# Moving scaling rows between VectorE and ScalarE in a row-normalizing kernel, tile by tile, with more buffers for the row sums

## The chip, the cores and the metric

One core of a Trainium2 chip. The metric is the device time of one execution in microseconds, median of several. The span in a profile, from the first instruction to the last, is 1.6 to 2.1 us shorter than the time of the same execution, by an amount that hardly changes within a kernel (1.6 for before, 1.8 for after).

The names in the profile lines: DVE is VectorE, ACT is ScalarE, POOL is GpSimd; SP is SyncE, whose queue issues the loads; ACTq is the queue of ScalarE, which issues the stores. L61 is line 61 of the kernel. A transfer is *issued* when its instruction runs, and has *landed* when the last of the core's 16 DMA engines reports its part. DMA engines move packets, here 49,152 bytes each (one partition's 12 rows) or 32,768 in the last tile; a full packet is one of 49,152.

## The reference

```python
x = np.random.randn(32, 512, 1024).astype(np.float32)
sums = np.sum(np.abs(x), axis=-1, keepdims=True)
return (x / (sums + 1e-8)).astype(np.float32)
```

16,384 rows of 1,024 numbers: 67.11 MB are read and 67.11 MB written, and each row is divided by the sum of its magnitudes.

## The kernel before

Each of the 128 partitions takes 128 rows, in tiles of 12 rows (6.29 MB over all partitions), with one last tile of 8 rows (4.19 MB). There are 11 tiles, numbered 0 to 10 here. `piece` picks a tile's rows in memory. Four tile buffers go round, so load i+4 waits until store i has landed. The code below is cut at the dots.

```python
R = 12; BUFS = 4; HEAD = 32
rows = [R] * ((per_partition - HEAD) // R + 2) + [HEAD - 2 * R]   # 12 x 10, then 8
sbuf  = ctx.enter_context(tc.tile_pool(name="sbuf", bufs=BUFS))
stats = ctx.enter_context(tc.tile_pool(name="stats", bufs=4))

def normalize(x_tile, r0, k, kv):
    s = stats.tile([P, R], FP32)
    nc.vector.tensor_reduce(out=s[:, :k], in_=x_tile[:, r0:r0+k, :], ...)   # sum of magnitudes
    # ... + EPS, then inv = 1 / s ...
    nc.vector.tensor_mul(out=x_tile[:, r0:r0+kv, :], ...)    # rows 0 to kv-1 on VectorE
    for r in range(kv, k):                                   # the rest on ScalarE, row by row
        nc.scalar.activation(out=row, in_=row, func=Copy, scale=inv[:, r:r+1])

for i, k in enumerate(rows):
    x_tile = sbuf.tile([P, R, d], FP32)
    nc.sync.dma_start(out=x_tile[:, :k, :], in_=piece(x_flat, i))       # load
    if i == 0:
        normalize(x_tile, 0, k, k - 5)                                  # 5 rows on ScalarE
    else:
        normalize(x_tile, 0, k, k - 1 if i + BUFS < len(rows) else k)   # 1 row, or none
    nc.scalar.dma_start(out=piece(out_flat, i), in_=x_tile[:, :k, :])   # store
```

Of the kernel before, what the change touches and what calls it, by code (L numbers as in the profile page):

```python
# [1 line left out]

# [4 lines left out]

FP32 = mybir.dt.float32
EPS = 1e-8


@with_exitstack
def kernel(
    ctx: ExitStack,
    tc: tile.TileContext,
    x: bass.AP,
    out: bass.AP,
):
    nc = tc.nc
    P = nc.NUM_PARTITIONS  # L20

    x_flat = x.flatten_outer_dims()
    out_flat = out.flatten_outer_dims()
    n, d = x_flat.shape




    R = 12
    BUFS = 4  # L30
    HEAD = 32
    per_partition = n // P
    assert n % P == 0 and (per_partition - HEAD) % R == 0
    rows = [R] * ((per_partition - HEAD) // R + 2) + [HEAD - 2 * R]

    def piece(flat, i):
        head = flat[: P * HEAD, :].rearrange("(p r) d -> p r d", p=P)
        if i < 2:
            return head[:, R * i : R * (i + 1), :]
        if i == len(rows) - 1:  # L40
            return head[:, 2 * R :, :]
        a = P * (HEAD + R * (i - 2))
        return flat[a : a + P * R, :].rearrange("(p r) d -> p r d", p=P)

    sbuf = ctx.enter_context(tc.tile_pool(name="sbuf", bufs=BUFS))
    stats = ctx.enter_context(tc.tile_pool(name="stats", bufs=4))

    def normalize(x_tile, r0, k, kv):

        s = stats.tile([P, R], FP32)  # L50
        nc.vector.tensor_reduce(  # L51
            out=s[:, :k],
            in_=x_tile[:, r0 : r0 + k, :],
            axis=mybir.AxisListType.X,
            op=mybir.AluOpType.add,
            apply_absolute_value=True,
        )
        nc.vector.tensor_scalar_add(out=s[:, :k], in0=s[:, :k], scalar1=EPS)  # L58
        inv = stats.tile([P, R], FP32)
        nc.vector.reciprocal(out=inv[:, :k], in_=s[:, :k])  # L60
        nc.vector.tensor_mul(  # L61
            out=x_tile[:, r0 : r0 + kv, :],
            in0=x_tile[:, r0 : r0 + kv, :],
            in1=inv[:, :kv].unsqueeze(2).to_broadcast([P, kv, d]),
        )
        for r in range(kv, k):
            row = x_tile[:, r0 + r, :]
            nc.scalar.activation(  # L68
                out=row,
                in_=row,  # L70
                func=mybir.ActivationFunctionType.Copy,
                scale=inv[:, r : r + 1],
            )

    with tc.manual_schedule():
        for i, k in enumerate(rows):
            x_tile = sbuf.tile([P, R, d], FP32)
            nc.sync.dma_start(out=x_tile[:, :k, :], in_=piece(x_flat, i))  # L78


            if i == 0:
                normalize(x_tile, 0, k, k - 5)
            else:
                normalize(x_tile, 0, k, k - 1 if i + BUFS < len(rows) else k)
            nc.scalar.dma_start(out=piece(out_flat, i), in_=x_tile[:, :k, :])  # L85


# [1 line left out]
_INS = ['x']  # L89
_OUTS = [((32, 512, 1024), 'float32')]  # L90


# [23 lines left out]
```

## Time and profile before

| | before |
|---|---|
| time, median of the first three runs | 317.26 us (316.87 to 317.87) |
| span of the first profile (an execution of 318.93 us) | 317.3 us |
| VectorE busy | 268.7 us, 85% |
| ScalarE busy | 13.5 us, 4% |
| moved by DMA | 134.22 MB, both directions |
| the 16 DMA engines: share of the span that packets took | 49.6% loads, 48.9% stores |

Loads and stores together filled 98.5% of the DMA engines' time. That is the first thing to read: VectorE's 85% is high too, but it has holes, and DMA has none. The profile has three views of the same end, and they are easily confused. The chain of work says who released whom. The timeline says when a store was issued. Only the landing and packet records say when the DMA engines got to it.

### The profile page before, as it was taken

What the parts mean: (1) busy time and instruction counts of PE and PEld (TensorE: products, weight loads), DVE (VectorE), ACT (ScalarE), POOL (GpSimd) and SP (SyncE); (2) the same over time, 40 slices, a digit from 0 to 9 for tenths busy, and PEclk for the clock granted to TensorE, in tenths of its full rate; (3) what the DMA queues carried; (4) which work ended last, traced back from release to release, by engine and by line L of the source; (5) the groups of instructions that cost most, each with busy time, mean ns of one, the idle gap of its engine ahead of it and who ended that gap; (6) DMA issues with size and microseconds to landing.
All of it is one profiled execution on the core that took longest, in us unless ns stands there. A gap on an engine that the chain in (4) does not pass through costs nothing.

```text
span 317.3 us, 170 instructions
## 1 busy us (share of the span) xinstructions
DVE 268.7 (85%) x44; ACT 13.5 (4%) x12; POOL 0.2 (0%) x4
## 2 busy tenths in 40 slices
DVE  0079999999999999989995996799699969999920
ACT  0010601001000000100100010000000000000000
POOL 0000000000000000000000000000000000000000
DMA  8999999999999999999999999999999999999994
GB/s 328 465 397 471 421 378 415 415 465 409 459 434 397 477 415 415 465 409 459 428 403 477 409 428 452 409 471 415 403 477 415 428 430 452 397 477 415 403 425 215
DMA packets 3168, 134.22 MB, mean 423 GB/s; under 512 B 352, under 2 KB 352, under 8 KB 352
## 3 DMA queue, kind: packets, MB, share of 16 engines
q1 hardware_dynamic: 1584, 67.11, 49.6%
q10 hardware_dynamic: 1584, 67.11, 48.9%
HBM read 67.11 MB, written 67.11 MB: 423 GB/s over the span
## 4 chain that ended last, share of the span: by engine, by line
DVE 52%; DMA 34%; another core or an unknown queue 9%; issue 0%; SPq 0%; DVEq 0%; ACTq 0%
DVE s L51 27%; DVE x_tile L61 24%; DMA x_tile<-in_x_dram 18%; DMA out_dram<-x_tile 16%; DVE inv L60 1%; DVE s L58 0%; SPq L78 0%; DVEq L60 0%; ACTq L85 0%
## 5 line engine op out<-in xcount | busy, mean ns | idle before, releaser
L51 DVE TENSOR_REDUCE s<-x_tile 128x12 f32<-128x12288 f32 (+1 forms) x11 | 138.2, 12561 | 32.9 <-DMA x_tile<-in_x_dram 32.9
L61 DVE TENSOR_TENSOR x_tile<-x_tile,inv 128x11264 f32<-128x11264 f32 (+3 forms) x11 | 126.5, 11504 | 0.4
L68 ACT ACTIVATE x_tile<-x_tile,inv 128x1024 f32<-128x1024 f32 x11 | 12.2, 1142 | 153.6 <-DVE inv L60 153.6
L60 DVE RECIPROCAL inv<-s 128x12 f32<-128x12 f32 (+1 forms) x11 | 2.5, 226 | 0.9
L58 DVE TENSOR_SCALAR s<-s 128x12 f32<-128x12 f32 (+1 forms) x11 | 1.9, 173 | 0.4
L68 ACT ACT_TABLE_LOAD x1 | 1.3, 1283 | 17.8 <-DMA x_tile<-in_x_dram 17.8
L100 POOL MEMSET const-bfloat16-1.0<- 128x1 bf16 x1 | 0.1, 102 | 0.0
L100 POOL MEMSET const-uint8-127<- 128x1 uint8 x1 | 0.1, 102 | 0.0
L100 POOL MEMSET const-float32-0.0<- 128x1 f32 x1 | 0.1, 99 | 0.2 <-issue 0.2
L100 POOL MEMSET const-float32-1.0<- 128x1 f32 x1 | 0.1, 99 | 0.0
## 6 DMA issues: line engine op xcount, KB each, us to landing
x_tile<-in_x_dram SPq DMA_DIRECT2D x10, 6144.0 KB, 39.2
out_dram<-x_tile ACTq DMA_DIRECT2D x10, 6144.0 KB, 43.7
x_tile<-in_x_dram SPq DMA_DIRECT2D x1, 4096.0 KB, 35.4
out_dram<-x_tile ACTq DMA_DIRECT2D x1, 4096.0 KB, 13.0
```

The lines of the kernel that those rows point to most:

```text
L51: nc.vector.tensor_reduce(out=s[:, :k], in_=x_tile[:, r0 : r0 + k, :], axis=mybir.AxisListType.X, op=mybir.AluOpType.add, apply_absolute_v ...
L58: nc.vector.tensor_scalar_add(out=s[:, :k], in0=s[:, :k], scalar1=EPS)
L60: nc.vector.reciprocal(out=inv[:, :k], in_=s[:, :k])
L61: nc.vector.tensor_mul(out=x_tile[:, r0 : r0 + kv, :], in0=x_tile[:, r0 : r0 + kv, :], in1=inv[:, :kv].unsqueeze(2).to_broadcast([P, kv, d]),)
L68: nc.scalar.activation(out=row, in_=row, func=mybir.ActivationFunctionType.Copy, scale=inv[:, r : r + 1],)
L100: nc = _bacc.Bacc("TRN2", target_bir_lowering=False, num_devices=1)
```

## The change

ScalarE's help moves to both ends of the kernel: three rows instead of one on tiles 1 and 2, two and three on the last two tiles, none in the middle. The intent is to issue early stores and the last stores sooner. The row sums get one buffer a tile, so that no tile waits for the sums of an earlier one to be read.

```diff
-    stats = ctx.enter_context(tc.tile_pool(name="stats", bufs=4))
+    stats = ctx.enter_context(tc.tile_pool(name="stats", bufs=len(rows)))
...
+    last = len(rows) - 1
+    scalar_rows = {0: 5, 1: 3, 2: 3, last - 1: 2, last: 3}
...
-            if i == 0:
-                normalize(x_tile, 0, k, k - 5)
-            else:
-                normalize(x_tile, 0, k, k - 1 if i + BUFS < len(rows) else k)
+            normalize(x_tile, 0, k, k - scalar_rows.get(i, 0))
```

## The prediction

> **What bounds the kernel now.** I number the tiles 0 to 10 in the order of the loop: ten of 12 rows per partition (6.29 MB each way), the last of 8 rows (4.19 MB). I read the page's slices first, then the bytes by stretch, then the chain of work, then the groups and the timeline.
>
> The 40 slices of the page, and what HBM moved:
>
> ```profile
> DVE  0079999999999999989995996799699969999920
> ACT  0010601001000000100100010000000000000000
> DMA  8999999999999999999999999999999999999994
> HBM read 67.11 MB, written 67.11 MB: 423 GB/s over the span
> ```
>
> DMA is at 9 in every slice but the first and the last; VectorE has holes from the middle on; ScalarE is nearly empty. Next, the stretches (after the range: its length, busy time of VectorE, ScalarE, GpSimd, the clock, the DMA share, GB/s):
>
> ```profile
> 32.00:40.00 8.00, 8.00 (x2) 4.52 (x5) 0.00 (x0) 1.00 0.91 393
> 40.00:48.00 8.00, 8.00 (x1) 0.00 (x0) 0.00 (x0) 1.00 1.05 387
> 192.00:224.00 32.00, 27.52 (x5) 0.00 (x0) 0.00 (x0) 1.00 1.02 441
> 288.00:302.00 14.00, 13.83 (x4) 0.00 (x0) 0.00 (x0) 1.00 1.04 449
> 302.00:306.00 4.00, 1.17 (x1) 0.00 (x0) 0.00 (x0) 1.00 0.66 279
> 306.00:314.00 8.00, 0.00 (x0) 0.00 (x0) 0.00 (x0) 1.00 0.94 406
> ```
>
> These rates wobble because a packet is 49 KB. Spreading each packet record over its own duration gives, in slices of 8 us, 433.6 to 434.1 GB/s nearly everywhere, whether loads run alone, both directions, or stores alone; a full packet takes 1815 ns on its DMA engine. So 134.22 MB at 433.8 GB/s is 309.4 us that no instruction order shortens. The first packet starts at 1.73 us: together 311.1. The other 6.2 us of the 317.3 us span, by my addition over the packet records: 0.9 slow first packets, 1.3 slow packets when the first store starts (40 to 48 us: 365 instead of 433.8 GB/s), about 0.4 scattered slow ones, 0.5 a gap before the last store, 1.8 DMA engines that finish unevenly (13 of 16 near 313.9, the last at 315.88), 1.4 after the last packet.
>
> The chain of work tells another story, and one must not fall for it:
>
> ```profile
> 258.85 12.96 DVE s L51
> 272.38 12.96 DVE x_tile L61
> 285.33 8.61 DVE s L51
> 294.48 8.69 DVE x_tile L61
> ```
>
> It follows releases: load 9 lands at 258.83, VectorE works through tiles 9 and 10, the last store is issued at 303.2 and lands at 316.23. It doesn't show that this store then queues behind the one before. The landing records do: store 9 has its last landing at 306.56, store 10 at 316.23. The 9.67 us between are exactly 4.19 MB at 433.8 GB/s. The DMA engine that ends last had no idle time before store 10.
>
> **What the Trainium skill says.** "DMA: Bandwidth & Descriptors", section "Where 436 GB/s comes from", puts the ceiling of the fabric at 435.2 GB/s; 433.8 measured agrees. The same section says that about 358 GB/s of HBM binds such transfers; this trace disagrees. "SBUF — State Buffer", section "Who interferes with whom", says that neither ScalarE nor a DMA contends with VectorE. The trace agrees for ScalarE: the multiply of 7 rows beside five ScalarE rows took 7626 ns, and 12 rows without took 12958, which is 1066 ns a row at one fixed cost. "ScalarE: Activation LUTs", section "What ACT_TABLE_LOAD costs", gives 280 + 0.833 N ns for an activation with one per-partition pointer operand, so 1133 for 1024 elements, and 93 ns of overlap back to back; the trace has 1142, and five in 5.30 us. [...]
>
> **The change part by part.** The prices are in these groups:
>
> ```profile
> L61 DVE TENSOR_TENSOR x_tile<-x_tile,inv 128x11264 f32<-128x11264 f32 x6 | 71.4, 11892 | 0.2
> L61 DVE TENSOR_TENSOR x_tile<-x_tile,inv 128x12288 f32<-128x12288 f32 x3 | 38.9, 12958 | 0.1
> L68 ACT ACTIVATE x_tile<-x_tile,inv 128x1024 f32<-128x1024 f32 x11 | 12.2, 1142 | 153.6 <-DVE inv L60 153.6
> ```
>
> Rows on ScalarE were 5 on tile 0, one on each of tiles 1 to 6, none after. They become 5, 3, 3, then none on 3 to 8, 2 on tile 9, 3 on tile 10: 16 instead of 11. VectorE loses five rows in all, 5 x 1.066 = 5.3 us of its 268.7; ScalarE gains 5.5.
>
> - Tile 0: nothing changes. Its store is still issued at 38.9 and still meets the slow packets after it.
> - Tiles 1 and 2: two rows fewer, multiply 11.89 - 2.13 = 9.76 us; ScalarE's three rows (about 3.3) lie beside it. Store 1 is issued at 62.1 instead of 64.19, store 2 at 85.2 instead of 89.45. But store 0 lands only at 73.29 and store 1 at 102.3; the queue is full, and the stores land when they did. Loads 4 to 6, which wait for these landings to get their buffers back, do not move either.
> - Tile 3: its load landed at 82.87, VectorE is ready at 85.1; multiply 12.96 instead of 11.89; store 3 at about 111.5 instead of 114.7. Tile 4 then waits some 0.5 us for its load (111.87); store 4 at about 138.4 instead of 140.0.
> - Tiles 5 and 6: they start where their loads land (141.07, 170.20), which does not move. The multiply is 1.07 longer, so stores 5 and 6 are issued at 167.7 and 196.8 instead of 166.6 and 195.7. Stores 4 and 5 before them land at 189.3 and 218.3, so there are over 20 us of reserve: 0 us.
> - Tiles 7 and 8: as before.
> - Tile 9: starts with its load at 258.85; multiply 12.96 - 2.13 = 10.83; store 9 at 283.25 instead of 285.37. Store 8 lands at 292.08: 0 us.
> - Tile 10: its load's landing, about 283.0, is just earlier than VectorE's being free at 283.2. Reduction 8.68, small ones about 0.5, multiply of 5 rows 8.69 - 3 x 1.066 = 5.49; store 10 at about 298.0 instead of 303.2, 5.2 us earlier. What that is worth is the question. Thirteen of the 16 DMA engines had a gap of 0.26 to 0.89 us at 303.3 to 303.8 us, as they were done with store 9 and the last store was not there (the 279 GB/s of 302 to 306). These gaps close, 0.5 us on the average engine. The other three, with the one that ends last among them, had store 10 waiting behind store 9; for them an earlier issue changes nothing. So the end moves by 0 if that engine is equally late, and by up to 0.5 in runs where it is less so. I put 0.2.
> - Buffers of the row sums: 11 instead of 4 of each kind. VectorE's reciprocal of tile 4 and later waits for ScalarE's read of tile i-4, over long before; the trace has only an extra sequencer step of 0.07 us ahead of it. Seven of these are 0.5 us on VectorE, off the path: 0 us.
>
> Sum: 317.26 - 0.2 = 317.06, say **317.0 us**.
>
> **The rivals.** First: *the chain is right*, VectorE's tail sets the end. Then the 5.2 us at the end count in full and the time is 317.3 - 5.2 = 312 us, 1.6% faster. For it speaks the chain, which runs over VectorE from 258.85 to 303.2. Against it: 312 would leave less than a microsecond over the 311.1 of bytes and first packet, with slow packets of over 2 us and 1.4 after the last packet still to pay; and the 9.67 us between the last two landings.
> Second: *VectorE becomes the bound in the middle*, since tiles 3 to 6 get their row back: 4 x 1.07 = 4.3 us, so 321.5, 1.3% slower. Against it: VectorE's work for a full tile is then 12.95 + 12.96 + 0.6 = 26.5 us, and a tile's 12.58 MB take 29.0 us of DMA. Tiles 7 and 8 already run this way, with waits of 4.3 and 2.9 us for their loads:
>
> ```profile
> 199.95 12.95 DVE L51 TENSOR_REDUCE s<-x_tile 128x12 f32<-128x12288 f32 x1 [4.31 <-DMA x_tile<-in_x_dram]
> 229.38 12.95 DVE L51 TENSOR_REDUCE s<-x_tile 128x12 f32<-128x12288 f32 x1 [2.94 <-DMA x_tile<-in_x_dram]
> ```
>
> Third: *the moved stores change the slow packets*. The last engine's 2 us of lateness come from single slow packets near the landings of stores (187, 217, 246 us), whose cause I can't read. With stores 1 to 6 issued one to four microseconds differently, this may go either way: 316.2 to 318. I can't exclude it, and it makes most of my range.
>
> **Range and chances.** The three runs before lie within 1.0 us (316.87 to 317.87). Adding the third rival and up to 0.5 us of closed gap, I take 316.2 to 317.9. 2% is 6.3 us: faster by that would be 310.9, under the 311.1 of the bytes alone, so 0.01; slower by it would need VectorE to starve the store queue, against reserves of 9 us and more: 0.01. Within 2%: 0.98.
>
> **What would show it right or wrong.** Right: VectorE about 263.4 us busy; ScalarE 16 activations; the last store issued near 298 and taking some 18 instead of 13.0 us to land; no dip at 302 to 306; first loads' landings as before; the last landing within 0.7 us of 316.2. Wrong in the first step, if the last landing comes over 1 us earlier: then the issue of the last store did set the end. Wrong in the middle, if a store is issued later than the one before it lands, or the DMA share falls between 100 and 280 us. If the span changes by a microsecond with none of this, it is the uneven DMA engines.

## More of the kernel before

Most executions agree within a fraction of a percent; a few are one to three and a half microseconds longer.

## The result, and the profile after

After: **316.62 us** median (316.45 to 317.59, six runs). Before, with the first three runs counted in: 316.78 us (316.46 to 317.87, six runs). The ratio is **0.9998**, 95% interval 0.9976 to 1.002: the same. Ratios here are the mean time of one kernel's runs over that of the other's of the same rounds, so they are not quite the ratio of the medians quoted.

The 40 slices of the page after:

```profile
DVE  0079999999999999969996998899699969999400
ACT  0010603004000000000000000000000000202100
DMA  8999999999999999999999999999999999999996
HBM read 67.11 MB, written 67.11 MB: 425 GB/s over the span
```

ScalarE's digits have moved to the ends, VectorE's row ends about one slice earlier, and the DMA row is unchanged except for its last digit. The stretches after (columns as in the prediction: length, busy VectorE, ScalarE, GpSimd, clock, DMA share, GB/s):

```profile
40.00:48.00 8.00, 8.00 (x1) 0.00 (x0) 0.00 (x0) 1.00 1.06 393
288.00:302.00 14.00, 7.37 (x4) 3.23 (x3) 0.00 (x0) 1.00 1.01 439
302.00:306.00 4.00, 0.00 (x0) 0.00 (x0) 0.00 (x0) 1.00 0.87 377
306.00:314.00 8.00, 0.00 (x0) 0.00 (x0) 0.00 (x0) 1.00 0.92 397
```

The dip at 302 to 306 has gone from 279 to 377 GB/s, and VectorE is done by 296. (A window counts a packet where it starts. With each packet spread over its duration, 296 to 304 us has 434 GB/s after, and had 411 before.) The four big steps of the chain at the end (start, duration, what), and what the page's list of DMA issues says of the last store (size, us from issue to landing), before and then after:

```profile
256.62 12.96 DVE s L51
270.08 10.83 DVE x_tile L61
280.91 8.61 DVE s L51
289.98 5.49 DVE x_tile L61
```

```profile
out_dram<-x_tile ACTq DMA_DIRECT2D x1, 4096.0 KB, 13.0
```

```profile
out_dram<-x_tile ACTq DMA_DIRECT2D x1, 4096.0 KB, 19.3
```

Both multiplies are shorter, by 2.13 and 3.20 us, and VectorE's tail ends 7.7 us sooner than in the first profile of before; the other 2.2 to 2.4 us are tile 9's load, which landed at 256.6 instead of 258.8. The last store is issued at 295.6 instead of 303.2, and then takes 19.3 us instead of 13.0 to land. Of the 7.7 us won at the issue, 6.3 are lost in the queue.

The groups of the multiplies, with their prices (busy us, mean ns, idle before):

```profile
L61 DVE TENSOR_TENSOR x_tile<-x_tile,inv 128x12288 f32<-128x12288 f32 x6 | 77.7, 12958 | 0.4
L61 DVE TENSOR_TENSOR x_tile<-x_tile,inv 128x9216 f32<-128x9216 f32 x2 | 19.5, 9758 | 0.1
```

Nine rows cost 9758 ns, as worked out beforehand from 7, 11 and 12 rows (9.76). The middle tiles, back at 12958, still wait for their loads:

```profile
198.64 12.95 DVE L51 TENSOR_REDUCE s<-x_tile 128x12 f32<-128x12288 f32 x1 [2.55 <-DMA x_tile<-in_x_dram]
```

So this profile agrees with the explanation by bytes. But the span is 1.5 us shorter than that of the first profile, and the last landing comes at 314.9 instead of 316.2. Either the tail counted a little after all, or the first profile was of a long execution. That had to be told apart.

### The profile page after: what moved, and what is told of

It is laid out like the page before. It is cut to its first block, busy times and chain, and to the rows that moved or that the text cites. A ratio compares the mean times of both kernels' runs of the same rounds, so it can differ in the third digit from the quotient of the medians.

```text
span 315.8 us, 162 instructions
## 1 busy us (share of the span) xinstructions
DVE 263.4 (83%) x44; ACT 18.5 (6%) x17; POOL 0.2 (0%) x4
## 4 chain that ended last, share of the span: by engine, by line
DVE 42%; DMA 33%; another core or an unknown queue 18%; SPq 0%; issue 0%
DVE s L51 23%; DVE x_tile L61 18%; DMA x_tile<-in_x_dram 17%; DMA out_dram<-x_tile 16%; DVE inv L60 0%; DVE s L58 0%; SPq L83 0%
## 5 line engine op out<-in xcount | busy, mean ns | idle before, releaser
L61 DVE TENSOR_TENSOR x_tile<-x_tile,inv 128x12288 f32<-128x12288 f32 (+4 forms) x11 | 121.2, 11019 | 0.6
L68 ACT ACTIVATE x_tile<-x_tile,inv 128x1024 f32<-128x1024 f32 x16 | 17.2, 1138 | 257.0 <-DVE inv L60 257.0
## 6 DMA issues: line engine op xcount, KB each, us to landing
out_dram<-x_tile ACTq DMA_DIRECT2D x1, 4096.0 KB, 19.3
```

The costliest lines, as they stand in the source:

```text
L61: nc.vector.tensor_mul(out=x_tile[:, r0 : r0 + kv, :], in0=x_tile[:, r0 : r0 + kv, :], in1=inv[:, :kv].unsqueeze(2).to_broadcast([P, kv, d]),)
L68: nc.scalar.activation(out=row, in_=row, func=mybir.ActivationFunctionType.Copy, scale=inv[:, r : r + 1],)
```

## The experiments

Three theories. **A**: the bytes set the time, and a store only has to be issued before the one ahead of it has drained. **B**: VectorE's work or its tail sets it, as the chain suggests. **C**: what differs is the DMA engines' scattered slow packets, whatever the order. A fourth, **D**, came out of the second run. "The kernel before" in each comparison was run in the same rounds: medians 316.81, 317.16 and 317.21 us for the three groups of four kernels each (on chips 0, 12 and 7), in the order they ran.

### Only the tail of the change

```diff
-                normalize(x_tile, 0, k, k - 1 if i + BUFS < len(rows) else k)
+                normalize(x_tile, 0, k, k - {9: 2, 10: 3}.get(i, 1 if i + BUFS < len(rows) else 0))
```

> The kernel before, with only the tail of the change: ScalarE takes 2 rows of tile 9 and 3 of tile 10. Theory A (the bytes set the time; the last store only has to be issued before the store ahead of it has drained): last store issued near 298 instead of 303.2 us, time within 0.6 us of the kernel before. Theory B (the chain of work is right, VectorE's tail sets the end): about 5.2 us shorter, near 311.6.

Measured: 317.96 us, ratio 1.0045 (1.0016 to 1.0073). The last store was issued at 295.4:

```profile
295.41 0.34 ACTq L85 DMA_DIRECT2D out_dram<-x_tile  x1
```

Theory B, which wanted 311.6, is out. The time is 1.1 us over before, which is more than the 0.6 that A allowed, and in the wrong direction for B. The profiled execution (317.33 us, the shortest of the six) doesn't show the excess: its last landing, 314.4, is earlier than that of either profile of before. I come back to this under the four buffers.

### The last store later, in two steps

A 4-row, then an 8-row reduction of tile 10 whose result nobody reads goes in front of tile 10's own work, in the kernel before:

```diff
+    def burn(x_tile, m):
+        nc.vector.tensor_reduce(out=junk[:, :m], in_=x_tile[:, :m, :], ...)
...
+            if i == len(rows) - 1:
+                burn(x_tile, 4)        # 8 in the second kernel
```

> The kernel before, with a further 4-row reduction of tile 10 on VectorE, its result unused, so that the last store is issued 4.4 us later, near 307.6. Theory A: the DMA engines have drained the store before by about 303.5 to 304, so nearly all of it shows: 3.5 to 4.4 us slower, 320.3 to 321.2. Theory B: 4.4 us slower too. The run tells, with the tail-only run, whether the effect of the last store's issue has a knee: none before about 303 us, full after it.

> As the run before with 8 rows: the last store is issued 8.8 us later, near 312. Theory A: 7.9 to 8.8 us slower, 324.7 to 325.6; the step from the 4-row run is 4.3 to 4.4 us in full.

Measured: 319.39 us (ratio 1.0086, +2.6 us) and 323.57 us (1.0238, +6.8 us). The step between them is 4.2 us, as expected, but the first is 1 to 2 us too small. The traces say why: the last stores were issued at 305.1 and 309.3, not at 307.6 and 312. Without the added 4.4 us, this execution would have issued at about 300.7, not at the 303.2 of the first profile. Tile 9's load had landed at 256.4, not at 258.8. The stretch 302 to 306, from the 4-row and the 8-row run:

```profile
302.00:306.00 4.00, 3.02 (x1) 0.00 (x0) 0.00 (x0) 1.00 0.33 143
```

```profile
302.00:306.00 4.00, 4.00 (x1) 0.00 (x0) 0.00 (x0) 1.00 0.17 74
```

Now the DMA engines stand still: by the packet records, 1.9 to 2.8 us on every one of the 16 in the 4-row run, 6.0 to 7.1 in the 8-row run. In the 4-row run they were done with store 9 between 303.3 and 304.0 us, and the last store's first packet came 0.8 us after its issue. The deadline for issuing is thus about 303.3 - 0.8 = 302.5 us. An ordinary execution issues at 300.7, with 1.8 us to spare, and 4.4 - 1.8 = 2.6 us is what was measured. (That it fits to the digit is luck: the ratio's interval is 1.9 to 3.6 us wide.)

### The kernel before and the kernel after, again

> The kernel before against itself: the ratio of identical programs, 1.000, and how far it strays; two earlier runs were 0.4% over. And a second profile: if the late DMA engine of the first profile was an accident of that execution, load 9 lands near 256.4 and the last store is issued near 300.8 instead of 303.2, with no gap before it.

> The kernel after again, in the same rounds as the kernel before against itself: within 0.4% of it. If it is 0.4% faster than the run with four buffers of row sums was, relative to the kernel before, the buffers may matter; if its ratio is about 1.002 to 1.004, they do not.

Measured: 317.13 us, ratio 0.9989 (0.9948 to 1.0031) for before against itself; 316.97 us, ratio 0.9989 (0.9946 to 1.0032) for after. By the expectation's own rule this leaves it that the buffers may matter: after is 0.5% faster, relative to before, than the run with four buffers of row sums (1.0040). That is taken up in the section on four buffers. The second profile of before confirms the accident. Its timeline has tile 10 about 2.2 us earlier than the first profile had it, the dip is not there, and the last store is issued at 301.0:

```profile
283.04 8.68 DVE L51 TENSOR_REDUCE s<-x_tile 128x8 f32<-128x8192 f32 x1
292.26 8.69 DVE L61 TENSOR_TENSOR x_tile<-x_tile,inv 128x8192 f32<-128x8192 f32 x1
```

```profile
302.00:306.00 4.00, 0.00 (x0) 0.00 (x0) 0.00 (x0) 1.00 0.87 377
```

The 377 GB/s are those of the kernel after, to the digit: no DMA engine had a gap ahead of the last store in either. The first profile was of an execution of 318.93 us, longer than every one of the unprofiled ones quoted with it.

The second profile of after, of an execution of 318.58 us, shows the same scatter from the other side. Its load 9 lands at 258.0, its last store is issued at 297.4, still early enough that no DMA engine has a gap, and yet its last landing, 315.9, comes later than that of before's second profile (315.3). In these four profiles what differs most is how late the last DMA engine is. It ends 1.8 us (before, first), 1.1 (before, second), 0.7 (after, first) and 1.95 us (after, second) behind the mean of the 16. Put in one table, the last store's issue against the time:

| kernel | last store issued (profile), us | time, us | ratio to before |
|---|---|---|---|
| tail only | 295.4 | 317.96 | 1.0045 |
| after | 295.6 | 316.62 | 0.9998 |
| after, second profile | 297.4 | 316.97 | 0.9989 |
| before, second profile | 301.0 | 317.13 | 0.9989 |
| before + 4 rows | 305.1 | 319.39 | 1.0086 |
| before + 8 rows | 309.3 | 323.57 | 1.0238 |

Flat up to 301 within half a percent, and slope one from 305.1 to 309.3. No run lies between 301 and 305; that the bend is at about 302.5 is the estimate above.

### More work on VectorE in the middle

The kernel after, with an unused reduction of 2, then 4 rows in each of tiles 3 to 8:

```diff
+            if 3 <= i <= 8:
+                burn(x_tile, 2)        # 4 in the second kernel
```

> The kernel after, with a further 2-row reduction on VectorE, its result unused, in each of tiles 3 to 8: 6 x 2.2 = 13.2 us more VectorE work. Theory A: a full tile then takes VectorE 28.7 us, just under the 29.0 us of its bytes, so nothing is lost: within 0.6 us of the kernel after, though VectorE's waits for loads nearly vanish. Theory B (VectorE bounds the middle): several us up to 13 us slower.

> The same with 4 rows: 6 x 4.4 = 26.2 us more VectorE work, 30.9 us a tile against 29.0 us of bytes. Theory A: VectorE falls behind by 1.9 us a tile, which the backlog of stores hides until tile 8; store 9 is issued near 294 us, after store 8 has drained near 289, and the time is some 5 to 6 us longer, near 322. Theory B: most of the 26 us.

Measured: 317.13 us (ratio 1.0020, 0.9991 to 1.0049) and 322.03 us (1.0158). The first added 13.7 us of VectorE work and cost nothing that can be seen. Its list of waits has VectorE waiting for one load only, the first (in all, times, longest):

```profile
DVE s L62 <- DMA x_tile<-in_x_dram: 17.7, 1, 17.7
```

The second added 26.5 us and cost about 5: it issued store 9 at 293.5, after store 8 had landed at 289.7, and for 5 us nothing was left to move:

```profile
288.00:294.00 6.00, 6.00 (x2) 0.00 (x0) 0.00 (x0) 1.00 0.00 0
```

A's working hit both. VectorE's slack in the middle is real and lies between 2.3 and 4.4 us a tile, and what runs out first is the backlog of stores.

### Fewer bytes

```diff
-            nc.scalar.dma_start(out=piece(out_flat, i), in_=x_tile[:, :k, :])
+            ks = 6 if i == 5 else k
+            nc.scalar.dma_start(out=piece(out_flat, i)[:, :ks, :], in_=x_tile[:, :ks, :])
```

> The kernel after, with half of tile 5's store left out (6 of 12 rows, 3.15 MB); the result is wrong on purpose. Theory A: 3.15 MB at 433.8 GB/s is 7.25 us, so near 309.3, 2.3% faster, with VectorE's work unchanged. Theory B (VectorE or its tail is the bound): much less than that.

Measured: 309.34 us, ratio 0.9763 (0.9747 to 0.9780), wrong result. That is 7.8 us under the kernel before of the same rounds (317.16), and 7.3 under the kernel after in its own (316.62): the bytes left out, at the full rate. VectorE did the same work. This is the positive side of A: 2.3% of the bytes are 2.3% of the time.

### Four buffers for the row sums

```diff
-    stats = ctx.enter_context(tc.tile_pool(name="stats", bufs=len(rows)))
+    stats = ctx.enter_context(tc.tile_pool(name="stats", bufs=4))
```

> The kernel after, with 4 buffers of the row sums again. Theory A: no change, within 0.6 us; only sequencer steps of about 0.1 us ahead of some VectorE instructions come back.

Measured: 317.99 us, ratio 1.0040 (1.0013 to 1.0067). As with the tail-only kernel, this is 0.4% more than A allowed, and its interval excludes 1. The profile offers no cause in the kernel's order. VectorE's extra sequencer steps are 0.07 us each, the last store is issued at 296.8 us, well in time, and no DMA engine has a gap ahead of it. What its packet records show are scattered slow packets, such as 422 instead of 434 GB/s from 216 to 224 us. The kernel before, which has four buffers too, came out at 0.9989 against itself, but with an interval of 0.4% either way. Some of the 0.4% is not in the kernel's span at all. The time outside the span is 2.0 to 2.2 us in the six runs with four buffers, and 1.6 to 1.7 us in before's of the same rounds, so 0.5 us of the 1.2 us between the means; the spans differ by 0.3 us in the median and 0.8 in the mean. Why the part outside differs is not shown. In the tail-only kernel it explains only 0.2 us. Four buffers alone don't cost it, as the kernel before has them; four buffers together with several ScalarE rows on a tile, which both of these kernels have and before only on tile 0, were not separated from scatter. So I can't tell 0.4% from the scatter of executions here: inconclusive, at most about half a percent.

### ScalarE scales nothing

```diff
-    scalar_rows = {0: 5, 1: 3, 2: 3, last - 1: 2, last: 3}
+    scalar_rows = {}
```

> The kernel after, with ScalarE scaling no row at all, so that the first store is issued near 44 instead of 38.9 us, and VectorE is busy 281 instead of 263 us. Theory A: the loads keep the DMA engines busy until about 60 us, every later store is still issued before the one ahead of it has landed: time within 0.6 us of the others. Theory B (VectorE's work sets the time): up to 17.6 us slower, at least the 5.3 us of the first tile or of the tail. Theory C (uneven slow packets): a change of up to 1 us either way that shows in no store's issue.

Measured: **324.06 us**, ratio 1.0219 (1.0191 to 1.0247), 7.3 us slower. Theory A as it stood failed here. VectorE was not the reason in the way B has it: on tiles 7 to 9 it waited 2.2 to 2.9 us for each load again. The DMA engines were busy, but slow. From 48 to 96 us the three stretches of 16 us have 390, 399 and 399 GB/s. Summed over the packet records, packets that took longer than the ordinary 1815 ns between 38 and 112 us cost 4.9 us per DMA engine, where the kernels before and after lose 1.2 to 1.3. That is 3.6 us more on the average engine. Gaps ahead of the last store add some 0.7 us on the average engine; the rest is unevenness. Most engines ended near 317.6 us, the last at 320.5, and that one had no gap ahead of the last store (issued at 306.9), though ten others had, of up to 2.5 us.

So a theory **D**: what ScalarE's rows on the first tile buy is not VectorE time but the early first store, and a later first store meets slow packets. Two runs separate the first tile from the rest, and the store from VectorE:

```diff
-    scalar_rows = {0: 5, 1: 3, 2: 3, last - 1: 2, last: 3}
+    scalar_rows = {1: 3, 2: 3, last - 1: 2, last: 3}
```

> The kernel after, with the first tile's five rows back on VectorE; the other rows of the change stay. First store issued near 44.2 instead of 38.9 us. The run without any ScalarE rows lost 7.3 us; its packet records put about 5 of them in slow packets between 44 and 96 us. Theory D (what ScalarE buys is the early first store: it is under way before the loads run out of buffers, and later than that packets are slow while both directions start): most of the 7.3 us come back here, 320 to 323 us. Theory A as it stood: within 0.6 us of the kernel after.

```diff
+            if i == 0:
+                for _ in range(7):
+                    nc.scalar.activation(out=hold, in_=x_tile[:, k - 1, :], func=Copy)
             nc.scalar.dma_start(out=piece(out_flat, i), in_=x_tile[:, :k, :])
```

> The kernel after, with nothing changed on VectorE, but the first store held back by seven unused activations on ScalarE, so that it too is issued near 44. Theory D: it loses about as much as the run with the first tile on VectorE, 4 us or more, though VectorE is as early as in the kernel after. If VectorE's lateness was the cause, the time is within 0.6 us of the kernel after.

Measured: **321.83 us** (ratio 1.0158, 1.0104 to 1.0213; by the medians 4.6 us over the kernel before of these rounds) with the first tile on VectorE, and **323.64 us** (1.0191, 1.0148 to 1.0235; 6.4 us) with only the first store held back. In the second, VectorE's second tile starts as early as ever; only the store is late. The first store's issue in the kernel after, then the timeline with it held back:

```profile
38.87 0.38 ACTq L85 DMA_DIRECT2D out_dram<-x_tile  x1
```

```profile
36.60 7.58 ACT L89 ACTIVATE hold<-x_tile 128x1024 f32<-128x1024 f32 x7
38.80 12.94 DVE L53 TENSOR_REDUCE s<-x_tile 128x12 f32<-128x12288 f32 x1
43.13 0.37 ACTq L94 DMA_DIRECT2D out_dram<-x_tile  x1
```

A first store 4.3 us later costs about 6 us. The stretches of the kernel after, then those with the first store held back:

```profile
48.00:64.00 16.00, 15.90 (x5) 3.23 (x3) 0.00 (x0) 1.00 1.01 436
64.00:80.00 16.00, 15.90 (x4) 3.23 (x3) 0.00 (x0) 1.00 0.99 430
```

```profile
48.00:64.00 16.00, 15.90 (x5) 3.22 (x3) 0.00 (x0) 1.00 0.98 390
64.00:80.00 16.00, 15.90 (x4) 3.23 (x3) 0.00 (x0) 1.00 1.00 390
```

VectorE and ScalarE do the same in these stretches; only the DMA rate differs. The DMA share stays at one, so the loss cannot be seen in the share, only in the GB/s. With each packet spread over its duration:

| us | after: loads + stores, GB/s | first store held back: loads + stores |
|---|---|---|
| 40 to 48 | 245 + 122 = 367 | 398 + 0 = 398 |
| 48 to 56 | 175 + 259 = 434 | 213 + 197 = 410 |
| 56 to 64 | 211 + 223 = 434 | 175 + 195 = 370 |
| 64 to 72 | 251 + 183 = 434 | 186 + 193 = 380 |
| 72 to 80 | 235 + 199 = 434 | 147 + 252 = 400 |
| 80 to 88 | 169 + 265 = 434 | 5 + 409 = 414 |
| 88 to 96 | 220 + 215 = 434 | 194 + 186 = 381 |

In the kernel after, loads slow down once, in packets that start between 40.4 and 45.3 us, the first of them after the store's issue (38.9) and before its own first packet (43.3), and all is at full rate in the rest of the table. With the store held back, many packets of both directions are slow over some 40 us. Packets over the ordinary 1815 ns between 38 and 112 us cost 3.9 us per DMA engine with the first tile on VectorE and 5.1 with the store held back, against 1.2 in the kernel after; most of the rest is that the engines end unevenly (the first and the last are 4.8 and 3.7 us apart, and 1.3 in the kernel after). Then the loads run dry for a moment, since load 4 waits for the first store's landing (82.8 instead of 73.6), and when they start again there are slow packets again. As the DMA engines are busy from start to end, nothing makes up for this later. D holds as far as the first store's time goes.

Why these packets are slow is **open**. In the good cases the first store's packets begin at 43.2 us, in the middle of load 2, and load 3 begins after that. In the three bad cases they begin at 48.3 to 48.8 us, when load 2 is over (its last packets start at 44.6) and load 3 has begun (at 45.8 to 46.0), so store 0 and load 3 start within three microseconds of each other and run side by side. That is a correlation over three kernels, not a cause. Nor do the runs point to a kernel that beats both: what is left to win is the 1.2 us of slow packets at the first store and the uneven ends. A first store still earlier was not tried.

## Why the prediction was right or wrong, point by point

- **The bound.** Right in what sets the time, and shown by taking bytes away (7.3 to 7.8 us for 3.15 MB) and by adding 13.7 us of VectorE work for nothing.
- **Tiles 1 and 2.** Stores were issued at 62.0 and 85.1 (expected 62.1 and 85.2). The first two stores landed at 73.6 and 102.6, as against 73.3 and 102.3 in the first profile: the queue was full, and it bought nothing.
- **Tiles 3 to 6.** Stores at 111.4, 137.8, 167.2 and 196.1, expected 111.5, 138.4, 167.7 and 196.8. The rows given back to VectorE cost nothing. The second rival (321.5 us) fell.
- **The tail.** The step of the prediction that gave 0.2 us for "the gaps close" rested on a gap that is not there in general. The ratio of 0.9998 shows no gain, but its interval, some 0.7 us either way, could not show 0.2. "Thirteen of the 16 DMA engines had a gap of 0.26 to 0.89 us" was true of the one execution profiled, not of the kernel. In its second profile, the kernel before issues its last store at 301.0, 1.5 us ahead of the deadline, and there is no gap to close. The first rival, 312 us by the chain, fell with the tail-only run.
- **The test named for the first step was a bad one.** The prediction said that a last landing over 1 us before 316.2 would prove the issue of the last store to be what sets the end. It came at 314.9. But the second profile of before has it at 315.3 with the late issue, and the second of after at 315.9 with the early one: nothing of the 1.4 us can be put down to the kernels. A criterion finer than the spread of single executions can't be read from one profile each.
- **The buffers.** 0 expected. The one comparison shows 0.4 to 0.5% in favour of more buffers, and that was not resolved.
- **The third rival**, single slow packets, fits the difference between executions of one kernel: the last DMA engine's lateness varies from 0.7 to 1.95 us in four profiles, while slow packets summed over all engines cost 2.3 to 2.6 us in each. What makes these packets slow is not shown.
- **The number** is partly luck. Its start, 317.26, was the median of three runs; six gave 316.78. And the prediction took the span of 317.3 us apart as if it were that time, while this span is of an execution of 318.93 us. The time of 312 us of the first rival would be a span of about 310.3, and so below the 311.1 of bytes and first packet, not just above it: its argument was better than it knew.
- **What the prediction didn't see.** Its line on tile 0, "nothing changes", was right for this change. But it took the five rows there for just another few microseconds of VectorE time, and the middle argument, that order is free as long as both queues have work, was too strong. The time of the first store is worth 4.6 to 6.4 us, through the packets' speed. The change kept it; that is why it came out even.

## What to carry to other kernels

Where the DMA engines are busy from end to end and at full rate, as in most of this kernel, an earlier issue was only worth what it kept the queue from running dry, so compare a store's issue with the landing of the store ahead of it, not with the chain. Busy DMA is not the same as fast DMA: read the GB/s of short stretches, above all where the second direction starts. And before building on a gap of half a microsecond in one profile, take a second profile of the same kernel.

## What the Trainium skill lacked or had wrong

- "DMA: Bandwidth & Descriptors", section "Where 436 GB/s comes from": it says that for transfers between HBM and SBUF about 358 GB/s of HBM bind. Here one core held 433.8 GB/s in most of the kernel, with loads alone, stores alone and both. Its fabric ceiling of 435.2 is the number that fits. The same page's section "Measured (HBM→SBUF, 128 partitions, SWDGE, issued from GpSimd)" is nearer: it has 425 for one large load of a core alone, and gives about 358 to each core only when both cores of the HBM domain stream. One core ran here, so it is the flat sentence that is wrong for this case; two were not tried.
- The same page, section "Latency and other measured facts", gives some 600 ns to the first byte of a DMA issued from ScalarE's or SyncE's queue. Where the DMA engines stood idle, the last store needed 0.8 us from the start of its issue to its first packet (305.06 to 305.90 in the 4-row run). The first store, issued while loads ran, needed 4.3 us (38.9 to 43.2), and 5.7 where it was held back (43.1 to 48.8).
- No page that I read says that packets slow down where stores start beside running loads: full packets of loads took up to 3.2 us instead of 1.8 around 41 to 43 us in the profiles of both kernels. Nor that this can last: with the first store 4 to 5 us later, 370 to 417 GB/s from 48 to 96 us instead of 434, in runs that lost 4.6 to 7.3 us of the whole.
- "VectorE: DVE Perf Modes" has no duration of an fp32 multiply as long as these; its formula (N+151)/0.96 ns, checked there for an add of 512 and 2048 elements, comes within 3 ns of all the multiplies here (5492 ns for 5120 elements, 9758 for 9216, 12958 for 12288).
